# A pairwise scan's key products on another engine, its levels spaced wider, and one weight tile moved by 192 bytes, in a one-core encoder layer

## The chip, the core and the metric

The kernel runs on one core of a Trainium2 chip. The core has five engines that take their instructions in order, each from its own queue, and meet by semaphores: TensorE (PE in the profile; its weight loads are PEld), VectorE (DVE), ScalarE (ACT), GpSimd (POOL) and SyncE (SP), which issues most DMAs here. The metric is the device time of one execution in microseconds, the median of several runs.

## What is computed

One layer of an encoder over 512 tokens of width 1024, in float32. Three branches share one input projection; their results are gated and summed, and a SwiGLU feed-forward part (FFN) of width 2816 follows:

```python
h = rms_norm(x, norm1_g[l])
proj = h @ w_in[l]
u_pool, aq, ak, av, rq, rf, rb, ri, rg, gate_pre = split_cols(proj)
y_pool = pool_mixer(u_pool, pool_w[l], pool_scale[l])
y_attn = diff_attention(aq, ak, av, lam, diff_norm_g[l], lambda_init)
y_rec = hgrn2_mixer(rq, rf, rb, ri, rg, lb_all[0, l], lb_all[1, l], hgrn_norm_g[l])
...
x = x + merged @ w_out[l]
h2 = rms_norm(x, norm2_g[l])
gu = h2 @ w_ffn_in[l]
x = x + (jax.nn.silu(gu[..., :FFN_HIDDEN]) * gu[..., FFN_HIDDEN:]) @ w_ffn_out[l]
```

The branch that matters most here is `hgrn2_mixer`: for 4 heads, in both directions of time, a gated linear recurrence S_t = diag(f_t) S_(t-1) + k_t v_t with key k = 1 - f and output S_t^T q_t. Written without the state, token t weighs the value of token s with the sum over channels of q_t k_s times the product of the gates f between s and t.

## The kernel before, in words

**Precision.** Dense products are made as three passes in the fast format fp32r: activations and weights are each split into a high part and a rest, and high x high, rest x high and high x rest are added up in PSUM. A weight tile comes by DMA as `raw`, ScalarE casts it into `whi` (line 180), and VectorE subtracts to get `wlo` (line 181); `split_w` does this, for 128 x 1024 numbers at a time. Three pairs of such tiles exist at once (pool `wsp`).

**Order.** TensorE's order is fixed by the program, not by a scheduler. `Pipe` keeps a clock of TensorE that `mm` advances by a modelled time for each matmul (about 0.215 us for 512 columns), and switches between several generators. A generator that yields `("w", us)` is resumed no earlier than that many modelled microseconds later, and one that yields `("e", event, us)` that long after an event was marked. Meanwhile the stream of dense jobs (`Jobs.stream`) is served, which yields after every two matmuls. So a number in a `yield` says how many dense matmuls stand between two steps of a scan, and it is not a wait on the chip. The other engines get their instructions in the order in which this program writes them, with some reordering by the scheduler.

**Stages.** The recurrent branch comes first (to about 231 us), then attention (to 366), pooling and the gates and up-projections, the output projection (522 to 568), the FFN's first half in 22 pairs of column tiles (569 to 784) and its second (784 to 905).

**The scan.** `rec_scan(h)` computes one head's 512 x 512 weights by doubling: at level n = 1, 2, 4, ... 128 all pairs of tokens in neighbouring blocks of n get their weights from four matmuls of 128 columns (float32, each shown as two records), "rc<-kq,kc" in the profile, line 90. Their left operand up to n = 64 is `kc`, a copy of the keys with the two directions interleaved (`key_copy`, ScalarE, line 724); the right one is the queries in `kq`. Then the level prepares the next: the queries are multiplied by gate products (two instructions on VectorE, line 755), the keys likewise (one instruction, line 758, on GpSimd for n < 128 and on VectorE for n = 128), the next `key_copy` is made from them, the pyramid of gate products `pyr` grows by a step (VectorE, line 765), and the level's weights are copied under a mask into `pt` (VectorE, line 770). The last pair of blocks, n = 256, needs four matmuls of 256 columns. Every level ends with a yield of 2.0 modelled us, the last with 1.7 (line 774).

**Values jobs.** `values_job` makes the recurrent and the attention branch's values: for each half of 256 columns and each of 4 token blocks, 24 matmuls of 256 columns ("mm<-whi,hT_hi" and the like), whose moving operand is the weight tile and whose stationary one is the transposed input `hT`. `quarter_parts` names their weights.

**Attention.** `att_front_job` evacuates the keys of a head from PSUM, with low halves "l" at line 848, and marks the event `AF`; `att_head` begins its first scores 3.5 modelled us later (line 861).

**FFN pairs.** For each pair j of column tiles `ffn_pair_bodies` runs seven products of 12 matmuls of 256 columns. The activations there stand 192 bytes further on than a tile of a multiple of 256 would, by pads that the program allocates (`h2_a`, `forms_a`). In the first part of pairs 4 and 12 two more matmuls of 512 columns write a PSUM bank that nobody reads ("tp<-whi"; called dummy matmuls below).

Of the kernel before, what the change touches and what calls it, by code (L numbers as in the profile page):

```python
# [11 lines left out]
F32 = mybir.dt.float32  # L12
# [6 lines left out]
P = 128  # L19
# [57 lines left out]
def encoder_kernel(ctx: ExitStack, tc: tile.TileContext, x, norm1_g, w_in, pool_w, pool_scale,  # L77
# [32 lines left out]
    wsp = ctx.enter_context(pool("wsp", 3))  # L110
    small = ctx.enter_context(pool("small", 6))
    psum = ctx.enter_context(pool("psum", 3, space=PSUM))
# [17 lines left out]
    masks = const.tile([P, len(LEVELS), P], U8, name="masks")  # L130
    vecs = const.tile([14, P], F32, name="vecs")
    vcol = const.tile([P, 14], F32, name="vcol")
# [30 lines left out]
    class Part:  # L163


        def __init__(self, chunk, view, a, b, wpool=None):
            self.chunk, self.view, self.a, self.b, self.wpool = chunk, view, a, b, wpool
            chunk.left += 1
# [4 lines left out]
        def split(self):  # L173
            self.hi, self.lo = split_w(self.view(self.chunk.raw), self.a, self.b, self.wpool)
            self.chunk.left -= 1

    def split_w(view, a, b, wpool=None):
        hi = (wpool or wsp).tile([P, a, b], F32R, name="whi")
        lo = (wpool or wsp).tile([P, a, b], F32R, name="wlo")
        nc.scalar.copy(out=hi, in_=view)  # L180
        nc.vector.tensor_tensor(out=lo, in0=view, in1=hi.bitcast(F32), op=ALU.subtract)  # L181
        return hi, lo
# [205 lines left out]

    def quarter_parts(w, c0, n, where=None):

        v = w.rearrange("(kt p) c -> p kt c", p=P)
        for c in range(0, n, 256):
            ch = Chunk(v[:, :, c0 + c:c0 + c + 256], KT, 256, where if c == 0 else None)
            yield slice(c, c + 256), [Part(ch, lambda raw, j=j: raw[:, j:j + 4, :], 4, 256) for j in (0, 4)]

# [71 lines left out]
    xraw = st0.enter_context(pool("xraw", 3))  # L467
    g_b = xg.tile([P, D], F32, name="g1b")
    with tc.issue_after(warmed):
        nc.scalar.dma_start(out=g_b, in_=norm1_g.broadcast_to([P, D]))  # L470
# [238 lines left out]
    def rec_scan(h):  # L709
# [30 lines left out]
        while n < 256:  # L740
            nb2 = S // (2 * n)
            ps = bank("rc", (P, NB, P))
            for b in range(NB):
# [6 lines left out]
                mm(ps[:, b, :], ks, qs, True, True)  # L750

            for off, o in ((0, tstep + 1), (S + n, 0)):
                xv = strided(kq, off, [[2 * n, nb2], [1, n]])
                tv = strided(tot, toff + o, [[2, nb2], [0, n]])
                nc.vector.tensor_tensor(out=xv, in0=xv, in1=tv, op=ALU.mult)  # L755
            xv = strided(kq, 2 * S, [[2 * n, nb2], [S + n, 2], [1, n]])
            tv = strided(tot, toff + 1, [[2, nb2], [tstep - 1, 2], [0, n]])
            (nc.gpsimd if n < 128 else nc.vector).tensor_tensor(out=xv, in0=xv, in1=tv, op=ALU.mult)  # L758
            if n < 64:
                kc = key_copy(2 * n)  # L760
            if n < 128:
# [11 lines left out]
            n *= 2  # L773
            yield ("w", 2.0 if n <= 128 else 1.7)
        for d in range(2):
# [21 lines left out]
    cols["rg"] = col_parts(w_in2, KT, OFF["rg"], 512, P)  # L797
    vparts = list(quarter_parts(w_in2, OFF["ri"], 512))

# [58 lines left out]
    def att_head(h):  # L858
        if h:
            yield ("e", f"T{h - 1}", 0.0)  # L860
        yield ("e", f"AF{h}", 3.5)
        t = att.pop(h)
# [74 lines left out]
    add_att(1)  # L937
    aparts = list(quarter_parts(w_in2, OFF["av"], 512))
    for i, (cs, parts) in enumerate(aparts):
# [174 lines left out]
    def ffn_pair_bodies(j):  # L1114
# [3 lines left out]
        def first(part):  # L1118
# [7 lines left out]

            if j in (4, 12):
                w = part.hi.rearrange("p n k c -> p (n k c)")
                for skip in (0, 16):
                    mm(bank("tp"), w[:, 0:P], w[:, skip:skip + 512], True, True)  # L1130
# [241 lines left out]
```

## Time and profile before

| | us |
|---|---|
| median of 3 runs | 913.66 |
| lowest and highest | 913.07, 913.75 |
| the profiled execution | 913.64 |
| its span, first to last instruction | 911.9 |
| TensorE busy | 889.2 (98%) |
| VectorE busy | 582.0 (64%) |
| ScalarE busy | 420.7 (46%) |
| GpSimd busy | 62.0 (7%) |

The busy times are sums over the span and overlap each other, so they don't add up to it. An engine that is busy nearly all the time sets the time, unless its work can be made shorter or it waits less; of an engine that is seldom busy it matters only whether another one waits for its results. A timeline row gives a start, a duration and, in brackets, how long the engine had been idle before it and what ended that idle time. Since matmuls are pipelined, the duration of a row of matmuls is longer than the distance to the next row's start; times per matmul are best taken from starts.

### The profile page before, as it was taken

What the parts mean: (1) busy time and instruction counts of PE and PEld (TensorE: products, weight loads), DVE (VectorE), ACT (ScalarE), POOL (GpSimd) and SP (SyncE); (2) the same over time, 40 slices, a digit from 0 to 9 for tenths busy, and PEclk for the clock granted to TensorE, in tenths of its full rate; (3) what the DMA queues carried; (4) which work ended last, traced back from release to release, by engine and by line L of the source; (5) the groups of instructions that cost most, each with busy time, mean ns of one, the idle gap of its engine ahead of it and who ended that gap; (6) DMA issues with size and microseconds to landing.
All of it is one profiled execution on the core that took longest, in us unless ns stands there. A gap on an engine that the chain in (4) does not pass through costs nothing. (4 is left out here: it accounts for less than half of the span.)

```text
span 911.9 us, 13179 instructions
## 1 busy us (share of the span) xinstructions
PE 889.2 (98%) x5357; PEld 783.6 (86%) x5357; DVE 582.0 (64%) x876; ACT 420.7 (46%) x652; POOL 62.0 (7%) x62
## 2 busy tenths in 40 slices
PE   6999999999999999999999999999999999999996
PEld 5977987887898888778888898999999999888885
DVE  5696553663867765654325554998887888644544
ACT  5544423433655674332233424755655556533433
POOL 2233311210000000000000000000000000000000
PEclk9999999999999999999999999999999999999999
DMA  8322030314033213523334350153433434323312
GB/s 244 106 69 70 3 91 25 114 47 154 26 112 91 89 52 117 185 79 96 97 122 147 102 153 0 48 139 94 137 95 104 128 94 133 122 70 105 111 39 93
DMA packets 106313, 89.01 MB, mean 98 GB/s; under 512 B 2686, under 2 KB 93324, under 8 KB 106124
## 3 DMA queue, kind: packets, MB, share of 16 engines
q1 hardware_dynamic: 105532, 86.59, 31.0%
q10 hardware_dynamic: 720, 1.57, 0.5%
q8 instruction: 42, 0.69, 0.3%
q14 instruction: 19, 0.16, 0.1%
HBM read 86.06 MB, written 2.10 MB: 97 GB/s over the span
## 5 line engine op out<-in xcount | busy, mean ns | idle before, releaser
L181 DVE TENSOR_TENSOR wlo<-raw,whi 128x1024 fp32r<-128x1024 f32 (+1 forms) x146 | 170.2, 1169 | 165.5 <-PE mm L90 85.0
L180 ACT CAST whi<-raw 128x1024 fp32r<-128x1024 f32 (+1 forms) x146 | 143.7, 990 | 207.5 <-PE mm L90 122.1
L90 PE MATMUL mm<-hT_hi,whi 128*128 128x512 f32 (+1 forms) x440 | 110.7, 389 | 0.0
L90 PE MATMUL mm<-hT_hi,wlo 128*128 128x512 f32 (+1 forms) x440 | 108.3, 383 | 0.0
L90 PE MATMUL mm<-hT_lo,whi 128*128 128x512 f32 (+1 forms) x440 | 107.9, 382 | 0.0
L90 PEld LDWEIGHTS mm<-hT_hi,whi 128*128 128x128 f32 x440 | 79.2, 191 | 16.0 <-issue 1.9
L90 PEld LDWEIGHTS mm<-hT_lo,whi 128*128 128x128 f32 x440 | 79.2, 188 | 15.0
L90 PEld LDWEIGHTS mm<-hT_hi,wlo 128*128 128x128 f32 x440 | 78.9, 188 | 15.4 <-issue 1.0
L299 DVE TENSOR_TENSOR slo<-sums,shi 128x1024 fp32r<-128x1024 f32 x42 | 51.1, 1217 | 0.2 <-ACT shi L297 0.2
L297 ACT CAST shi<-sums 128x1024 fp32r<-128x1024 f32 x42 | 44.2, 1052 | 2.0 <-DVE sums L261 1.5
L758 POOL TENSOR_TENSOR kq<-kq,pyr 128x512 f32<-128x512 f32 x24 | 33.4, 1392 | 46.4 <-ACT kc L724 29.9
L90 PEld LDWEIGHTS rc<-kq,kc 128*128 128x128 f32 x224 | 29.7, 191 | 6.7 <-issue 2.4
L90 PE MATMUL rc<-kq,kc 128*128 128x128 f32 x224 | 32.1, 287 | 2.9 <-DVE kq L755 2.9
L755 DVE TENSOR_TENSOR kq<-kq,pyr 128x256 f32<-128x256 f32 x56 | 26.1, 507 | 13.1 <-PE rc L90 13.0
L724 ACT COPY kc<-kq 128x512 f32<-128x512 f32 x28 | 18.7, 667 | 30.1 <-POOL kq L758 19.0
L882 ACT ACTIVATE s<-s,mx 128x512 f32<-128x512 f32 x32 | 23.0, 720 | 16.2 <-DVE mx L880 16.0
L90 PE MATMUL mm<-fhi,slo 128*128 128x256 f32 x168 | 26.2, 278 | 0.5 <-DVE slo L299 0.5
L90 PE MATMUL mm<-y_hi,whi 128*128 128x512 f32 x96 | 26.4, 393 | 0.0
L90 PE MATMUL mm<-y_lo,whi 128*128 128x512 f32 x96 | 26.2, 392 | 0.0
L90 PE MATMUL mm<-fhi,shi 128*128 128x256 f32 x168 | 26.1, 277 | 0.1
L90 PE MATMUL mm<-flo,shi 128*128 128x256 f32 x168 | 25.9, 276 | 0.0
L90 PE MATMUL mm<-y_hi,wlo 128*128 128x512 f32 x96 | 25.9, 390 | 0.0
(255 smaller groups left out, 1812.0 us busy)
## 6 DMA issues: line engine op xcount, KB each, us to landing
raw<-in_w_ffn_in_dram SPq DMA_DIRECT2D x44, 512.0 KB, 5.2
raw<-in_w_in_dram SPq DMA_DIRECT2D x18, 1024.0 KB, 5.1
raw<-in_w_in_dram SPq DMA_DIRECT2D x24, 512.0 KB, 4.1
raw<-in_w_ffn_out_dram SPq DMA_DIRECT2D x10, 1024.0 KB, 5.1
raw<-in_w_out_dram SPq DMA_DIRECT2D x4, 1024.0 KB, 5.4
xin<-in_x_dram SPq DMA_DIRECT2D x4, 512.0 KB, 9.4
raw<-in_w_up_rec_dram SPq DMA_DIRECT2D x2, 1024.0 KB, 7.9
x<-in_x_dram SPq DMA_DIRECT2D x1, 2048.0 KB
```

Source lines behind the costliest of these rows:

```text
L90: i = nc.tensor.matmul(out_, lhsT=lhsT, rhs=rhs, start=start, stop=stop, skip_group_check=chain)
L180: nc.scalar.copy(out=hi, in_=view)
L181: nc.vector.tensor_tensor(out=lo, in0=view, in1=hi.bitcast(F32), op=ALU.subtract)
L297: nc.scalar.copy(out=hi, in_=view)
L299: on_dve = nc.vector.tensor_tensor(out=lo, in0=view, in1=hi.bitcast(F32), op=ALU.subtract).ins
L724: nc.scalar.copy(out=strided(kc, 0, [[2 * n, S // (2 * n)], [n, 2], [1, n]]), in_=strided(kq, 2 * S, [[2 * n, S // (2 * n)], [S + n, 2], [ ...
L755: nc.vector.tensor_tensor(out=xv, in0=xv, in1=tv, op=ALU.mult)
L758: (nc.gpsimd if n < 128 else nc.vector).tensor_tensor(out=xv, in0=xv, in1=tv, op=ALU.mult)
L882: nc.scalar.activation(out=s, in_=s, func=AF.Exp, scale=-1.0, bias=mx[:, c:c + 1], accum_out=zz[:, i, c:c + 1])
```

## The change

1. In a level of the scan, the key product goes to VectorE for all n. It is written ahead of the two query products, and `key_copy` right behind it.
2. The yields between levels become 2.7 and 2.4 modelled us.
3. The weights of the values jobs (recurrent `ri` and attention `av`) begin 192 bytes into their tile; for that `wsp` tiles hold 1088 numbers instead of 1024.
4. The first scores of an attention head follow the event `AF` by 4.4 instead of 3.5.
5. The dummy matmuls stay at j = 4 only.
6. The pool of small tiles has 5 buffers instead of 6, and `vecs` lives in a pool of the first stage. With this all the tiles allocated behind `wsp` on that side move by a multiple of 256 bytes.

```diff
-    small = ctx.enter_context(pool("small", 6))
+    small = ctx.enter_context(pool("small", 5))
...
-    vecs = const.tile([14, P], F32, name="vecs")
...
-    def split_w(view, a, b, wpool=None):
-        hi = (wpool or wsp).tile([P, a, b], F32R, name="whi")
-        lo = (wpool or wsp).tile([P, a, b], F32R, name="wlo")
+    def split_w(view, a, b, wpool=None, skip=0):
+
+        n, k = a * b, skip // 4
+        hi, lo = ((wpool or wsp).tile([P, n if wpool else 1088], F32R, name=name)[:, k:k + n]
+                  .rearrange("p (a b) -> p a b", a=a) for name in ("whi", "wlo"))
         nc.scalar.copy(out=hi, in_=view)
         nc.vector.tensor_tensor(out=lo, in0=view, in1=hi.bitcast(F32), op=ALU.subtract)
...
+    vecs = xg.tile([14, P], F32, name="vecs")
...
+            xv = strided(kq, 2 * S, [[2 * n, nb2], [S + n, 2], [1, n]])
+            tv = strided(tot, toff + 1, [[2, nb2], [tstep - 1, 2], [0, n]])
+            nc.vector.tensor_tensor(out=xv, in0=xv, in1=tv, op=ALU.mult)
+            if n < 64:
+                kc = key_copy(2 * n)
             for off, o in ((0, tstep + 1), (S + n, 0)):
                 xv = strided(kq, off, [[2 * n, nb2], [1, n]])
                 tv = strided(tot, toff + o, [[2, nb2], [0, n]])
                 nc.vector.tensor_tensor(out=xv, in0=xv, in1=tv, op=ALU.mult)
-            xv = strided(kq, 2 * S, [[2 * n, nb2], [S + n, 2], [1, n]])
-            tv = strided(tot, toff + 1, [[2, nb2], [tstep - 1, 2], [0, n]])
-            (nc.gpsimd if n < 128 else nc.vector).tensor_tensor(out=xv, in0=xv, in1=tv, op=ALU.mult)
-            if n < 64:
-                kc = key_copy(2 * n)
...
-            yield ("w", 2.0 if n <= 128 else 1.7)
+            yield ("w", 2.7 if n <= 128 else 2.4)
...
-    vparts = list(quarter_parts(w_in2, OFF["ri"], 512))
+    vparts = list(quarter_parts(w_in2, OFF["ri"], 512, None, 192))
...
-        yield ("e", f"AF{h}", 3.5)
+        yield ("e", f"AF{h}", 4.4)
...
-    aparts = list(quarter_parts(w_in2, OFF["av"], 512))
+    aparts = list(quarter_parts(w_in2, OFF["av"], 512, None, 192))
...
-            if j in (4, 12):
+            if j == 4:
```

`quarter_parts` and `Part` hand the new argument `skip` on to `split_w`.

The order of the instructions differs from the one before in the stage of the scan, at the first scores of attention and at j = 12. Three places, with the rows of an engine as they stand in its queue. In these rows a name ahead of the arrow is what is written, the names behind it are what is read, and "x4" means four in a row.

TensorE at the end of head 0's scan, before: the three groups "rc<-..." are levels n = 64, n = 128 and the last pair of blocks, with dense matmuls "mm<-..." between them.

```order
L90 MATMUL rc<-kq,kc 128x128 x4
L90 MATMUL mm<-hT_hi,wlo 128x512 x8
L90 MATMUL mm<-hT_hi,whi 128x512 x2
L90 MATMUL rc<-kq 128x128 x4
L90 MATMUL mm<-hT_hi,whi 128x512 x6
L90 MATMUL mm<-hT_lo,whi 128x512 x2
L90 MATMUL rc<-kq 128x256 x4
```

The same place after the change.

```order
L90 MATMUL rc<-kq,kc 128x128 x4
L90 MATMUL mm<-hT_hi,wlo 128x512 x8
L90 MATMUL mm<-hT_hi,whi 128x512 x6
L90 MATMUL rc<-kq 128x128 x4
L90 MATMUL mm<-hT_hi,whi 128x512 x2
L90 MATMUL mm<-hT_lo,whi 128x512 x8
L90 MATMUL mm<-hT_hi,wlo 128x512 x2
L90 MATMUL rc<-kq 128x256 x4
```

Between the levels stand 14 and 12 dense matmuls where 10 and 8 stood.

VectorE at the first levels of head 0, before: "kc<-kq" is the sum of both directions' keys, "wlo" a weight split, "x2" at line 755 the two query products of a level, "pt" the masked copy, "pyr" a step of the gate products.

```order
L717 TENSOR_TENSOR kc<-kq 128x512
L181 TENSOR_TENSOR wlo<-raw,whi 128x1024
L755 TENSOR_TENSOR kq<-kq,f 128x256 x2
L770 COPY_PREDICATED pt<-masks,rc 128x4x128
L765 TENSOR_TENSOR pyr<-pyr 128x2x128
L765 TENSOR_TENSOR pyr<-pyr 128x2x64
L755 TENSOR_TENSOR kq<-kq,pyr 128x128x2 x2
L770 COPY_PREDICATED pt<-masks,rc 128x4x128
```

The same place after the change, where line 757 is the key product and line 763 the query product (768 is the pyramid, 773 the masked copy, 182 the split).

```order
L720 TENSOR_TENSOR kc<-kq 128x512
L757 TENSOR_TENSOR kq<-kq,f 128x256x2
L182 TENSOR_TENSOR wlo<-raw,whi 128x1024
L757 TENSOR_TENSOR kq<-kq,pyr 128x128x2x2
L768 TENSOR_TENSOR pyr<-pyr 128x2x128
L757 TENSOR_TENSOR kq<-kq,pyr 128x64x2x4
L763 TENSOR_TENSOR kq<-kq,f 128x256 x2
L773 COPY_PREDICATED pt<-masks,rc 128x4x128
```

Three levels' key products stand ahead of the first level's query products, since they need no matmul of their level.

TensorE at the first scores of attention, before: the four rows "rc<-k,q" and "rc<-l,q" are the scores (the numbers are those of the tiles), the others a dense job.

```order
L90 MATMUL mm<-hT_lo,whi 128x512 x8
L90 MATMUL mm<-hT_hi,wlo 128x512 x2
L90 MATMUL rc<-k_1865,q_1863 128x512
L90 MATMUL rc<-l_1867,q_1863 128x512
L90 MATMUL rc<-k_1866,q_1864 128x512
L90 MATMUL rc<-l_1868,q_1864 128x512
L90 MATMUL mm<-hT_hi,wlo 128x512 x6
```

The same place after the change.

```order
L90 MATMUL mm<-hT_lo,whi 128x512 x8
L90 MATMUL mm<-hT_hi,wlo 128x512 x6
L90 MATMUL rc<-k_1865,q_1863 128x512
L90 MATMUL rc<-l_1867,q_1863 128x512
L90 MATMUL rc<-k_1866,q_1864 128x512
L90 MATMUL rc<-l_1868,q_1864 128x512
L90 MATMUL mm<-hT_hi,wlo 128x512 x2
```

The scores stand four dense matmuls later.

## Rows read from the trace of the kernel before

**Rows 1.** Page, busy times of the engines and the granted clock in 40 slices.

```profile
PE 889.2 (98%) x5357; PEld 783.6 (86%) x5357; DVE 582.0 (64%) x876; ACT 420.7 (46%) x652; POOL 62.0 (7%) x62
...
PEclk9999999999999999999999999999999999999999
```

**Rows 2.** TensorE's waits: engine, line, waited for; us, times, longest.

```profile
PE rc L90 <- DVE kq L755: 3.5, 5, 1.0
...
PE rc L90 <- DVE kq L758: 1.4, 1, 1.4
PE rc L90 <- DVE l L848: 0.7, 1, 0.7
```

**Rows 3.** Timeline of TensorE, head 0's last levels: start, us, what, idle before.

```profile
64.76 1.13 PE L90 MATMUL rc<-kq 128*128 128x128 f32 x8 [0.52 <-DVE kq L755]
...
67.12 0.61 PE L90 MATMUL mm<-hT_lo,whi 128*128 128x512 f32 x2
69.14 1.97 PE L90 MATMUL rc<-kq 128*128 128x256 f32 x8 [1.41 <-DVE kq L758]
```

**Rows 4.** Timeline of VectorE, same stretch.

```profile
61.99 2.62 DVE L755 TENSOR_TENSOR kq<-kq,pyr 128x256 f32<-128x256 f32 x2
...
65.15 2.57 DVE L181 TENSOR_TENSOR wlo<-raw,whi 128x1024 fp32r<-128x1024 f32 x1
67.65 0.75 DVE L755 TENSOR_TENSOR kq<-kq,pyr 128x256 f32<-128x256 f32 x2
68.32 0.68 DVE L758 TENSOR_TENSOR kq<-kq,pyr 128x512 f32<-128x512 f32 x1
```

**Rows 5.** Groups of VectorE, 380 to 900 us: busy us, mean ns.

```profile
L181 DVE TENSOR_TENSOR wlo<-raw,whi 128x1024 fp32r<-128x1024 f32 x76 | 92.8, 1223 | 120.4 <-PE mm L90 61.1 <-ACT whi L180 59.1
```

**Rows 6.** Timeline of GpSimd, same stretch as rows 4.

```profile
62.22 2.11 POOL L758 TENSOR_TENSOR kq<-kq,f 128x512 f32<-128x512 f32 x1 [6.83 <-ACT whi L180]
65.11 1.52 POOL L758 TENSOR_TENSOR kq<-kq,pyr 128x512 f32<-128x512 f32 x1 [0.79 <-ACT kc L724]
```

**Rows 7.** Busy time in windows of the scan.

```profile
75.00:100.00 25.00, 24.13 (x153) 21.25 (x153) 21.28 (x39) 9.40 (x15) 11.06 (x7) 1.00 0.08 22
```

**Rows 8.** Timeline of TensorE, a values job in the scan.

```profile
95.32 1.12 PE L90 MATMUL mm<-wlo,hT_hi 128*128 128x256 f32 x8
96.28 1.06 PE L90 MATMUL rc<-kq,kc 128*128 128x128 f32 x8
```

**Rows 9.** Timeline of TensorE, FFN, pairs j=4 and j=12.

```profile
614.22 0.63 PE L90 MATMUL rc<-h_hi,wlo 128*128 128x256 f32 x4
614.69 0.64 PE L90 MATMUL tp<-whi 128*128 128x512 f32 x2
615.16 0.63 PE L90 MATMUL mm<-fhi,shi 128*128 128x256 f32 x4
...
691.33 0.63 PE L90 MATMUL tp<-whi 128*128 128x512 f32 x2
691.79 0.63 PE L90 MATMUL mm<-fhi,shi 128*128 128x256 f32 x4
```

**Rows 10.** Groups of GpSimd, whole span, by form.

```profile
L758 POOL TENSOR_TENSOR kq<-kq,pyr 128x512 f32<-128x512 f32 x24 | 33.4, 1392 | 46.4 <-ACT kc L724 29.9 <-DVE pyr L765 14.4 <-DVE kq L755 2.2
L758 POOL TENSOR_TENSOR kq<-kq,f 128x512 f32<-128x512 f32 x4 | 8.7, 2181 | 51.5 <-ACT whi L180 26.5 <-DVE kc L717 18.4 <-DVE sg L704 6.6
```

**Rows 11.** Groups of VectorE, 36 to 206 us, by form.

```profile
L181 DVE TENSOR_TENSOR wlo<-raw,whi 128x1024 fp32r<-128x1024 f32 x19 | 26.5, 1406 | 25.4 <-PE mm L90 14.8 <-ACT pt L735 6.0 <-ACT whi L180 2.8
...
L758 DVE TENSOR_TENSOR kq<-kq,pyr 128x512 f32<-128x512 f32 x4 | 2.7, 682 | 0.0
```

**Rows 12.** Timeline of TensorE, first attention scores.

```profile
231.88 0.39 PE L90 MATMUL rc<-k,q 128*128 128x512 f32 x1
232.92 0.50 PE L90 MATMUL rc<-l,q 128*128 128x512 f32 x1 [0.66 <-DVE l L848]
```

**Rows 13.** Timeline of VectorE, same place.

```profile
231.47 1.40 DVE L848 TENSOR_TENSOR l<-mm,k 64x512 fp32r<-64x512 f32 x2 [1.24 <-ACT k L846]
```

More of the change, by code (lines that the diff above doesn't have):

```diff
@@ L163, in encoder_kernel, with __init__ @@
     class Part:
-        def __init__(self, chunk, view, a, b, wpool=None):
-            self.chunk, self.view, self.a, self.b, self.wpool = chunk, view, a, b, wpool
+        def __init__(self, chunk, view, a, b, wpool=None, skip=0):
+            self.chunk, self.view, self.a, self.b, self.wpool, self.skip = chunk, view, a, b, wpool, skip
             chunk.left += 1
@@ L173, in split @@
         def split(self):
-            self.hi, self.lo = split_w(self.view(self.chunk.raw), self.a, self.b, self.wpool)
+            self.hi, self.lo = split_w(self.view(self.chunk.raw), self.a, self.b, self.wpool, self.skip)
             self.chunk.left -= 1
-    def split_w(view, a, b, wpool=None):
-        hi = (wpool or wsp).tile([P, a, b], F32R, name="whi")
-        lo = (wpool or wsp).tile([P, a, b], F32R, name="wlo")
+    def split_w(view, a, b, wpool=None, skip=0):
+        n, k = a * b, skip // 4
+        hi, lo = ((wpool or wsp).tile([P, n if wpool else 1088], F32R, name=name)[:, k:k + n]
+                  .rearrange("p (a b) -> p a b", a=a) for name in ("whi", "wlo"))
         nc.scalar.copy(out=hi, in_=view)
@@ L387, in row_parts, with quarter_parts @@
                 yield Part(ch, lambda raw, j=j: raw[:, j:j + 2, :], 2, 512, wpool)
-    def quarter_parts(w, c0, n, where=None):
+    def quarter_parts(w, c0, n, where=None, skip=0):
         v = w.rearrange("(kt p) c -> p kt c", p=P)
@@ L393, in quarter_parts @@
             ch = Chunk(v[:, :, c0 + c:c0 + c + 256], KT, 256, where if c == 0 else None)
-            yield slice(c, c + 256), [Part(ch, lambda raw, j=j: raw[:, j:j + 4, :], 4, 256) for j in (0, 4)]
+            yield slice(c, c + 256), [Part(ch, lambda raw, j=j: raw[:, j:j + 4, :], 4, 256, None, skip)
+                                       for j in (0, 4)]
     def cols_mm(ps, part, r, nk, sub=0, lo_col=0, n=512, r_lo_last=False):
```

## The prediction

> **What bounds the kernel now.** I read the page's busy shares first: TensorE works 98% of the span, the other engines at most 64% [rows 1]. So time can leave in two ways only: TensorE waits less, or a matmul takes less. The span is 911.9 us in a profiled execution of 913.64, so about 1.7 lies around it; the median shown is 913.66. All sums below start from 913.64 and need no correction to the median.
>
> The list of TensorE's waits says how much there is to win by waiting less [rows 2]. Apart from the start of the program, the largest entries are two of the scan's own: 3.5 us in five waits for the query products (line 755) and 1.4 us in one wait for a key product (line 758); then 0.7 us once for the attention keys' low halves (line 848). A wait costs a little more than its idle: two matmuls of 512 columns begin at 67.12, and at 0.227 us each the next could begin at 67.57; it begins at 69.14, which is 1.57 later where the profile counts 1.41 idle [rows 3]. So 0.16 more for each of the six: 4.9 + 6 x 0.16 = 5.9 us in the scan.
>
> Why does a query product come late? VectorE's timeline has two of them at 61.99 that took 2.62 us together, and two at 67.65 that took 0.75; a weight split at 65.15 took 2.57 [rows 4], where 76 of the same form later in the kernel averaged 1.223 [rows 5]. GpSimd was running a key product at 62.22 for 2.11 us and another at 65.11 for 1.52 [rows 6]. The long VectorE instructions are those that lie beside a GpSimd one. TensorE's waits at 64.76 and 69.14 [rows 3] follow these two pairs: 61.99 + 2.62 = 64.61, and after 65.15 + 2.57 = 67.72 come the last level's query pair and key product, 67.65 + 0.75 and 68.32 + 0.68, which end at 69.00. VectorE had no long queue of its own: it was busy 21.28 of 25 us in the fullest window that I read, with that stretching in it [rows 7].
>
> For matmul prices I compared start distances at one size, 256 columns. In the values job eight of them go from 95.32 to 96.28, 120 ns each [rows 8]. In the FFN four go from 614.22 to 614.69, 117.5 ns each, and after two dummy matmuls at 614.69 the pitch is shorter: between 615.16 and 691.33 stand 8 pairs of 7 products of 12 matmuls, 672 in 76.17 us, 113.4 ns each [rows 9]. In the values job both operands begin at the same offset modulo 256 bytes (32 and 32); in the FFN the moving operand stands 192 further on (224 and 32), by the pad that the kernel has there. The granted clock is at its upper level, 2.4 GHz, in all these slices [rows 1], so the difference is not the clock's.
>
> **Key products to VectorE.** Leaves GpSimd: 24 instructions of 1.392 us and 4 of 2.181, 42.1 us [rows 10]. Comes to VectorE: 28 at the 0.682 that its four of the same form take now [rows 11], 19.1 us. Leaves VectorE: the stretching. For the 19 splits in this stretch that is 19 x (1.406 - 1.223) = 3.5 us [rows 5, 11], and for a pair of query products like that of 61.99 it is 1.9. So VectorE gets at most 15.6 us more work in 170, on an engine that has 3.7 us of 25 free in a full window [rows 7], some 25 us in 170: no bound by sum. The question is order. At a level, the key product of n up to 64 needs the key copy of its own level (ScalarE) and not TensorE, since the matmuls read the copy; it runs early. Behind it on VectorE wait the query products, the pyramid step, the mask copy and now and then a split, so a key copy that is late behind a weight cast on ScalarE delays all of these.
>
> **Levels further apart.** The modelled gap goes from 2.0 to 2.7 us; between the last levels of head 0 stand 14 and 12 dense matmuls where there were 10 and 8. Four more at 0.227 give VectorE 0.91 us more. A level then has 14 x 0.227 = 3.2 us of cover, or 12 x 0.227 = 2.7; it needs a key product 0.68, two query products 0.75, and a split of 1.22 if one stands ahead: 2.65 if all of it waited for the level's matmuls, and only the queries do. I walked the changed order with these durations. The least room left is about 1.0 us, in head 0's last levels and in head 1 where two splits stand ahead of the queries at n=32, of which the first begins ahead of the level's matmuls. That says all six waits go; I leave 0.4 for what the walk cannot see, and give the residual 0 to 2.5. Term: -5.5 (-5.9 to -3.4). The cover is dense work that has to be done anyway, and the scan doesn't run out of it: a head begins when its front is done, and in the changed order 70 dense matmuls (15.9 us) still stand between the last step of head 3 and the first scores of attention, 72 in the order before. So the spacing costs nothing; if that cover were gone, each level would cost its 0.9 openly.
>
> **Attention's first scores.** The fourth score matmul could begin at 231.88 + 0.227 = 232.11 and begins at 232.92, and the next record is 0.11 longer [rows 12]; it waits for two evacuations at 231.47 that take 1.40 [rows 13]. The delay of 0.9 puts four more dense matmuls ahead, 0.91 us, and the evacuation ends at 232.87, before 233.02. Term: -0.9 (-0.8 to -0.9). Nothing is late next: the later scores run without a stop.
>
> **Value weights 192 bytes on.** 2 sets x 2 halves x 4 blocks x 24 = 384 matmuls go from offsets 32/32 to 224/32. No row shows this pair in this stage, so bounds from the nearest: 113.4 ns as after 615.16, or 117.5 as ahead of 614.69. That is 384 x 6.6 = 2.5 or 384 x 2.5 = 0.9; no row of 256 columns is above 120, so no loss. I take 115 between them: -1.9.
>
> The Trainium skill ("SBUF — State Buffer", section "SBUF: two separate sides") says the opposite: on the engines' side of SBUF only the port pair that VectorE and GpSimd share is contended for, and TensorE waits for nobody. By it an offset would be worth nothing and the term would be 0, which is R2 below. The trace has 120 against 113.4 for one size, so I follow the rows.
>
> **Dummy matmuls at j=12.** Two matmuls, 691.33 to 691.79, 0.46 us on TensorE's path [rows 9]. Term: -0.5 (-0.4 to -0.5). Whether the 113.4 ns hold without them is R3.
>
> **Priced at nothing.** One buffer fewer in the pool of small tiles: each is read within its block, and five are left. The tile of vectors goes to another pool; its four loads keep their place. Other tiles move by 768 bytes, a multiple of 256, so offsets that matter stay. GpSimd's remaining work (the powers in the norms) comes earlier, and nobody waits for it at present.
>
> **Sum.** 913.64 - 5.5 - 0.9 - 1.9 - 0.5 = 904.84, say 904.9.
>
> **Rivals.** *Waits stay by order (R1).* In-order VectorE has key product, splits and evacuations ahead of the queries; where the key copy is behind a cast on ScalarE, the queue stands. If half of the 5.9 stays: 913.64 - 2.95 - 3.3 = 907.4. For it: two levels whose room is only about 1 us. Against it: the waits now all lie beside stretched instructions. Chance 0.15.
> *The offset does nothing (R2)*, as if 120 ns came from the values job itself: 904.9 + 1.9 = 906.8. For it: no row isolates the offset. Chance 0.08.
> *The FFN falls back (R3).* The change does less than it says if the FFN pays for it. The step from 117.5 to 113.4 at 614.69 looks like a state that two dummy matmuls set. If the pair at j=4 no longer sets it and no second pair follows, the stretch from 615 to 784 goes at 0.470 per four instead of 0.4525: 169 x 3.9% = 6.5, so 911.4. Against it: their addresses modulo 256 do not change. Chance 0.04.
> *Slower: VectorE becomes the bound of the scan (R4).* A level with two splits ahead that all wait for its matmuls needs 0.68 + 0.75 + 2 x 1.22 = 3.87 against a cover of 2.7 to 3.2, some 0.9 late. If half of the 28 levels were so, the waits would be 14 x 0.9 = 12.6 in place of 5.9: 913.64 + 6.7 - 3.3 = 917.0. It turns into a loss where waits pass 5.9 + 3.3 = 9.2 us, 0.33 a level. For it: 21.28 busy of 25 in one window. Against it: the stretching that leaves, and that 19 splits stand in this stretch, few of them in pairs. Chance 0.06.
>
> **How the numbers follow.** Forecast 0.67, R1 0.15, R2 0.08, R3 0.04, R4 0.06. The low end: every term at its best is 9.8 us, 903.8, and 0.4 more if the slow state before 614.69 is shorter: 903.4. The high end: 3.4 + 0.8 + 0.9 + 0.4 = 5.5 off, 908.1, which takes in R2 and most of R1; 908.2. About 2 in 10 is left outside. A measurement here can tell some 0.2%, 1.8 us. Faster by more: forecast, R1, R2 and half of R3, 0.92; within: the other half of R3 and the mild part of R4, 0.04; slower: the rest of R4, 0.04.
>
> **What would show it.** Right: no entry above 0.5 us for the query products in TensorE's waits and none for line 848 at the first scores; VectorE's splits in the scan back at 1.22 mean; values matmuls eight in 0.91 to 0.94 us; after the pair at j=4 four in 0.4525. Wrong: query waits of 0.3 us or more at many levels (R4), few long ones behind splits (R1), values still at 0.96 for eight (R2), FFN at 0.47 (R3). What would upset the forecast most is a queue on VectorE that a late key copy holds, since everything of a level is behind it.

## The result, and the profile after

The changed kernel took 904.12 us (median of 13 executions, 903.43 to 911.20), the kernel before beside it 914.07 (13, 912.71 to 922.35): a ratio of 0.9888, 95% interval 0.9853 to 0.9923. The interval is wide because the executions of either kernel fall into two groups some 7 us apart: 903.43 to 904.35 (eight) and 910.79 to 911.20 (five) here, 912.71 to 914.07 (seven) and 920.02 to 922.35 (six) before. Group against group the change is -9.7 us (medians 903.91 against 913.65) and -9.8 (911.07 against 920.90). What the groups are is taken up in the section on them below. The profiled executions, 903.87 and 913.64 us, both belong to the lower group; their spans are 902.0 and 911.9. Forecast were 904.9 us, and 903.4 to 908.2.

Where the time went is read from the starts of TensorE's rows at six places that both kernels have: the scan's first level, attention's first score, the first pooled product, the output projection's first matmul, the FFN's first, and the FFN's second half. This is TensorE's timeline of the kernel before at these places (start, duration, what).

```profile
40.39 0.82 PE L90 MATMUL rc<-kq,kc 128*128 128x128 f32 x4
...
231.42 0.39 PE L90 MATMUL rc<-k,q 128*128 128x512 f32 x1
...
378.00 1.02 PE L90 MATMUL rc<-dpool,pw 128*128 128x512 f32 x2
...
522.33 0.87 PE L90 MATMUL mm<-whi,m_hi 128*128 128x256 f32 x6
...
568.91 0.62 PE L90 MATMUL mm<-h_hi,whi 128*128 128x256 f32 x4
...
784.28 0.39 PE L90 MATMUL rc<-whi,shi 128*128 128x512 f32 x1
```

And of the changed kernel; the row at 605.35 is the pair of dummy matmuls at j = 4, which stands at 614.69 in [rows 9].

```profile
40.29 0.99 PE L90 MATMUL rc<-kq,kc 128*128 128x128 f32 x5
...
224.39 0.39 PE L90 MATMUL rc<-k,q 128*128 128x512 f32 x1
...
368.74 1.02 PE L90 MATMUL rc<-dpool,pw 128*128 128x512 f32 x2
...
513.04 0.87 PE L90 MATMUL mm<-whi,m_hi 128*128 128x256 f32 x6
...
560.18 0.62 PE L90 MATMUL mm<-h_hi,whi 128*128 128x256 f32 x4
...
605.35 0.63 PE L90 MATMUL tp<-whi 128*128 128x512 f32 x2
...
774.46 0.39 PE L90 MATMUL rc<-whi,shi 128*128 128x512 f32 x1
```

| stretch of TensorE | before, us | after, us | difference |
|---|---|---|---|
| scan, to the first score | 191.03 | 184.10 | -6.93 |
| attention, to pooling | 146.58 | 144.35 | -2.23 |
| pooling, gates, up-projections | 144.33 | 144.30 | -0.03 |
| output projection | 46.58 | 47.14 | +0.56 |
| FFN to the dummies at j = 4 | 45.78 | 45.17 | -0.61 |
| from there to the FFN's second half | 169.59 | 169.11 | -0.48 |

The four dense matmuls that now stand ahead of the first scores (0.91 us) moved from the second stretch to the first, so the scan's own gain is 7.84 and attention's 1.32.

The list of TensorE's waits of the changed kernel has none of the three entries of [rows 2]; this is the whole list (engine, line, what for; us, times, longest). The first two belong to the program's start.

```profile
PE tp L98 <- DVE hrow L432: 7.3, 1, 7.3
PE rc L98 <- DVE hrow L432: 1.4, 1, 1.4
PE mm L90 <- DVE slo L300: 0.4, 1, 0.4
```

VectorE's groups in the scan, 36 to 206 us, by form (busy us, mean ns):

```profile
L182 DVE TENSOR_TENSOR wlo<-raw,whi 128x1024 fp32r<-128x1024 f32 x20 | 24.2, 1218 | 16.0 <-ACT whi L181 6.8 <-PE mm L90 4.4 <-ACT pt L784 3.8
...
L757 DVE TENSOR_TENSOR kq<-kq,pyr 128x512 f32<-128x512 f32 x28 | 19.1, 683 | 2.2 <-ACT kc L727 1.8
```

The splits average 1.218 us where they had 1.406 [rows 11], and the 28 key products 0.683. The window that was VectorE's fullest [rows 7] now reads as follows (TensorE busy 25.00 of 25.00, VectorE 17.87, GpSimd 0.00):

```profile
75.00:100.00 25.00, 25.00 (x187) 23.81 (x186) 17.87 (x35) 10.02 (x17) 0.00 (x0) 1.00 0.08 22
```

Of these 28 key products 24 are new on VectorE, and with them come the four of the first levels, which took 1.138 us each: 20.9 us of work more. Yet its busy time over the whole span grew by 4.3 us only (582.0 to 586.3), and in this window, which does not hold quite the same work in both kernels, it is 3.4 us lower: the stretched rows are gone, query products among them (0.507 us before, 0.420 now). The last levels of head 0, which began after 0.52 and 1.41 us of idle [rows 3], begin without any:

```profile
69.37 1.05 PE L90 MATMUL rc<-kq 128*128 128x128 f32 x8
...
72.99 1.67 PE L90 MATMUL rc<-kq 128*128 128x256 f32 x7
```

### The profile page after: what moved, and what is told of

The parts are those of the page before. It is cut to its first block, busy times and chain, and to the rows that moved or that the text cites. A ratio compares the mean times of both kernels' runs of the same rounds, so it can differ in the third digit from the quotient of the medians.

```text
span 902.0 us, 13155 instructions
## 1 busy us (share of the span) xinstructions
PE 885.1 (98%) x5355; PEld 782.7 (87%) x5355; DVE 586.3 (65%) x904; ACT 420.8 (47%) x652; POOL 19.4 (2%) x34
## 3 DMA queue, kind: packets, MB, share of 16 engines
q10 hardware_dynamic: 720, 1.57, 0.5%
## 4 chain that ended last, share of the span: by engine, by line
PE 94%; DVE 3%; DMA 1%; ACT 1%; issue 1%; POOL 0%; POOLq 0%; SPq 0%; ACTq 0%; DVEq 0%
PE mm L90 66%; PE rc L90 23%; PE tp L90 4%; PE tp L98 2%; DMA xin<-in_x_dram 1%; DVE hid L352 1%; DMA raw<-in_w_ffn_in_dram 0%; DVE flo L352 0%; DVE h_lo L451 0%; DVE wlo L182 0%; DVE slo L300 0%; DVE hrow L432 0%; PE rc L98 0%; ACT x L1218 0%; ACT hrow L426 0%
## 5 line engine op out<-in xcount | busy, mean ns | idle before, releaser
L182 DVE TENSOR_TENSOR wlo<-raw,whi 128x1024 fp32r<-128x1024 f32 (+1 forms) x146 | 166.5, 1144 | 154.9 <-PE mm L90 77.7
L763 DVE TENSOR_TENSOR kq<-kq,pyr 128x256 f32<-128x256 f32 x56 | 21.5, 420 | 25.6 <-PE rc L90 25.5
L90 PE MATMUL mm<-whi,hhi 128*128 128x512 f32 x66 | 25.7, 389 | 0.0
```

Source lines behind the costliest of these rows:

```text
L90: i = nc.tensor.matmul(out_, lhsT=lhsT, rhs=rhs, start=start, stop=stop, skip_group_check=chain)
```

## Experiments on the scan

Three kernels undo the two parts of the scan's change, together and singly.

**Both undone.** Key product on GpSimd again (for n < 128, but written ahead of the queries), spacing 2.0 and 1.7:

```diff
-            nc.vector.tensor_tensor(out=xv, in0=xv, in1=tv, op=ALU.mult)
+            (nc.gpsimd if n < 128 else nc.vector).tensor_tensor(out=xv, in0=xv, in1=tv, op=ALU.mult)
...
-            yield ("w", 2.7 if n <= 128 else 2.4)
+            yield ("w", 2.0 if n <= 128 else 1.7)
```

> The changed kernel with its scan as it was in two points: key product for n<128 back on GpSimd (still written ahead of the queries) and spacing 2.0/1.7. Everything else stays changed. Theory (GpSimd's product stretches the VectorE instructions beside it, and the narrow spacing doesn't cover that): TensorE waits of 4 to 6 us for kq are back, 4 to 6 us slower than the changed kernel, that is 908 to 910. Rival (the position ahead of the queries was what helped): no waits above 0.5 us, within 1 us of the changed kernel.

Measured: 912.63 us median (lower group 911.97 to 913.39). Its waits:

```profile
PE rc L90 <- DVE kq L763: 3.8, 5, 1.3
PE mm L90 <- ACT shi L298: 1.5, 1, 1.5
...
PE rc L90 <- DVE kq L757: 1.0, 1, 1.0
```

Six waits of 4.8 us are back, and the stretch from the scan's first level to the first score takes 190.91 us, 6.8 more than in the changed kernel. That is more than the 4 to 6 expected. The position ahead of the queries, which this kernel keeps, helped little: less the four dense matmuls that moved (0.91) and with the value weights' 0.76 put back, the stretch would be 190.76 us against 191.03 before, 0.3 less. The rest of the difference isn't the scan's: 0.8 us fell at the program's start and 1.5 in the FFN, where the cast of the second row stood behind another that waited 2.40 us for its weight load (0.92 in the changed kernel). The third kernel has this wait too (1.0 us), the other ten and the two under study don't. Why the load was later there was not found.

**Only the engine undone.** The first of the two edits alone; TensorE's order is that of the changed kernel.

> The changed kernel with the key product for n<128 back on GpSimd; spacing 2.7/2.4 stays, TensorE's order is unchanged. Theory 1 (both parts are needed, each covers some): VectorE's splits in the scan back at 1.35 to 1.4 us mean, TensorE waits 1 to 3 us in the scan, 905 to 907. Rival A (the spacing alone covers everything): the same stretching on VectorE but no waits, within 0.3 us of the changed kernel. Rival B (the engine is all): the whole 4 to 6 us come back.

Measured: 904.22 us median (four executions, 903.98 to 904.94). In TensorE's waits there is no entry for kq. VectorE's splits, and GpSimd's key products:

```profile
L182 DVE TENSOR_TENSOR wlo<-raw,whi 128x1024 fp32r<-128x1024 f32 x20 | 27.4, 1380 | 18.2 <-ACT whi L181 6.8 <-PE mm L90 4.5 <-ACT pt L784 3.8
```

```profile
L757 POOL TENSOR_TENSOR kq<-kq,pyr 128x512 f32<-128x512 f32 x24 | 29.6, 1234 | 59.4 <-ACT kc L727 45.9 <-DVE pyr L768 10.6 <-DVE kq L763 2.9
```

Rival A holds: GpSimd runs its 38 us of key products (29.6 and 8.4 for the four first levels), VectorE's splits are stretched (1.380 us), and TensorE waits for none of it. From the scan's first level to the first score it took 184.37 us against 184.10. With the wide spacing the move to VectorE is worth 0.3 us, if anything.

**Only the spacing undone.** The second edit alone; key products on VectorE.

> The changed kernel with spacing 2.0/1.7; key products stay on VectorE. Theory 1 (both parts are needed): VectorE's splits at 1.22 mean, but 10 dense matmuls are 2.27 us against 0.75 of queries and 1.22 of a split: TensorE waits 0.5 to 2.5 us in the scan, 0.5 to 3 us slower than the changed kernel. Rival B (the engine is all): no waits, within 0.3 us. Rival A (the spacing is all): 4 to 6 us come back.

Measured: 906.59 us median (lower group 905.19 to 906.92). Its waits:

```profile
PE mm L90 <- ACT shi L298: 1.0, 1, 1.0
PE rc L90 <- DVE kq L763: 0.6, 1, 0.6
```

VectorE's splits average 1.222 us, unstretched, and yet one wait of 0.6 us stays (the starts of TensorE's rows show a second of 0.26); the stretch to the first score is 185.33 us, 1.2 more than in the changed kernel, and 1.0 of the rest is the load in the FFN. So either edit alone takes most of the waits: the engine 5.6 of the 6.8 us that both undone cost, the spacing 6.5. They are two ways to the same gain, not two gains.

## Experiments on the other three terms

**Attention's first scores.**

```diff
-        yield ("e", f"AF{h}", 4.4)
+        yield ("e", f"AF{h}", 3.5)
```

> The changed kernel with attention's first scores 3.5 modelled us behind the event as before. Forecast's term: a wait of 0.65 to 0.7 us for line 851 (the low halves of the keys) at the first scores is back, 0.9 us slower: 904.8. Rival (with the scan's waits gone VectorE is earlier there, so that the wait doesn't come back): no difference.

Measured: 904.42 us median (904.19 to 904.59). TensorE's timeline at the first scores:

```profile
224.27 0.39 PE L90 MATMUL rc<-k,q 128*128 128x512 f32 x1
225.31 0.50 PE L90 MATMUL rc<-l,q 128*128 128x512 f32 x1 [0.66 <-DVE l L851]
```

The wait is back to the hundredth [rows 12]: 225.31 - 224.27 - 0.227 = 0.81. The median is 0.5 us above the changed kernel's lower group; in the trace scan and attention together take 0.8 us more (329.22 against 328.45). The rival falls.

**The offset of the value weights.** First at the tile's start, then 64 bytes on; the second has the instructions in the same order as the changed kernel.

```diff
-    vparts = list(quarter_parts(w_in2, OFF["ri"], 512, None, 192))
+    vparts = list(quarter_parts(w_in2, OFF["ri"], 512, None, 0))
...
-    aparts = list(quarter_parts(w_in2, OFF["av"], 512, None, 192))
+    aparts = list(quarter_parts(w_in2, OFF["av"], 512, None, 0))
```

> The changed kernel with the value weights at the start of their tile again (offsets 32/32 modulo 256). Theory: the 384 values matmuls go back from 117 ns to 120 ns, 1.2 us slower (the term of the forecast was 0.9 to 2.5), and nothing else moves. Rival (the offset does nothing, the 117 ns come from other tiles' places): values stay at 117 ns, no difference. Second rival: later stages change too, since the out projection has 118 ns in the changed kernel where it had 113 to 114 before, and the FFN ahead of pair 4 has 113 where it had 117; if the values jobs hand on what sets these, out goes back to 113 to 114 (-0.9 us) and the FFN ahead of pair 4 to 117 (+0.6 us).

> The changed kernel with the value weights 64 bytes into their tile (offsets 96/32 modulo 256) instead of 192 (224/32); the order of the instructions is the same. Theory 1 (what counts is only that the two offsets differ): the values matmuls stay at 117 ns or go to 113, as with 192, time as the changed kernel within 0.5 us. Theory 2 (the distance counts): a third pitch, or 120 ns as with offset 0 and 0.7 to 1.2 us slower.

Measured: 904.86 us median at offset 0 (lower group 904.60 to 905.09), 903.87 at 64 (903.58 to 903.87). TensorE's timeline in a values job at offset 0, then at 64:

```profile
93.30 1.12 PE L90 MATMUL mm<-whi,hT_lo 128*128 128x256 f32 x8
...
95.22 0.40 PE L90 MATMUL mm<-whi,hT_hi 128*128 128x256 f32 x2
```

```profile
93.41 1.10 PE L90 MATMUL mm<-whi,hT_lo 128*128 128x256 f32 x8
...
95.29 0.40 PE L90 MATMUL mm<-whi,hT_hi 128*128 128x256 f32 x2
```

And in the changed kernel, at 192, in the same job, on either side of a scan level:

```profile
93.04 1.07 PE L90 MATMUL mm<-whi,hT_lo 128*128 128x256 f32 x8
...
94.85 0.39 PE L90 MATMUL mm<-whi,hT_hi 128*128 128x256 f32 x2
...
96.68 1.10 PE L90 MATMUL mm<-whi,hT_lo 128*128 128x256 f32 x8
...
98.56 0.64 PE L90 MATMUL mm<-whi,hT_hi 128*128 128x256 f32 x4
```

Between the two rows of a pair stand 16 matmuls: 1.92 us at offset 0, 120 ns each; 1.88 at 64, 118 ns each; at 192 it is 1.81 ahead of the level, 113 ns each, and 1.88 behind it. By the starts of the single matmuls the recurrent values at 192 go on like this, 113.5 and 117.8 ns in turn in all their eight stretches between scan levels (115.6 on average), while at 64 all eight have 117.7 to 118.0. Attention's values have mostly the slower pitch at both (117.0 and 116.7 on average). Over the scan and attention the kernel at offset 0 took 0.76 and 0.40 us more than the changed one, 1.16 in all; the kernel at 64 bytes took 0.40 more and 0.10 less. So it counts that the offsets differ, which is worth 0.9 us at 64 bytes and 1.2 at 192, and in the scan the distance counts as well, by the one profile at 64. That the kernel at 64 bytes has the changed one's time all the same comes from its output projection (46.6 us against 47.1), which is taken up below. The output projection and the FFN ahead of j = 4 at offset 0 are as in the changed kernel (47.13 and 45.19 us), so the second rival falls.

**The second pair of dummies.**

```diff
-            if j == 4:
+            if j in (4, 12):
```

> The changed kernel with the second dummy pair at j = 12 back. Forecast's term: 0.46 us slower in the lower group, nothing else. Rival (the second pair is a second chance to leave 117.5 ns): the upper group lies only some 2.5 to 3.5 us above the lower one, since the pairs behind j = 12 run at 113 ns. Second rival (each pair flips the pitch): fast executions become slow behind j = 12.

Measured: 904.23 us median (903.91 to 904.48). From the dummies at j = 4 to the FFN's second half TensorE took 169.59 us, to the hundredth what it took before, and 0.48 more than without the pair. So the second pair did not flip the pitch, and the second rival falls. No execution of four lay in the upper group, so the first rival is not decided.

## Experiments on the two groups of executions

**No dummies at all** (`if j == 4` made never true).

> The changed kernel without any dummy matmuls (the pair at j = 4 is gone too). Executions of the changed kernel fall into two groups, 903.4 to 904.4 us and 910.8 to 911.2 us. Theory (the 7 us are the FFN's 256-column matmuls at 117.5 instead of 113.4 ns, and the dummy pair switches between the two): without the pair the FFN keeps the pitch with which it starts, so that the shares of the two groups change; in a profile with 113 ns ahead of pair 4, the rest of the FFN stays at 113 and the time is 0.5 us below the changed kernel's lower group; with 117.5 ahead, it stays at 117.5 and the time is 6.5 us above. Rival (the groups have another cause, another stage): the shares stay about 8 to 5, and the time falls by the pair's 0.46 us in both.

Measured: 902.83, 903.21, 903.97 and 910.62 us, and the profiled execution is the last of these. It is the only profile of an upper group other than those of the kernels with single dummies below:

```profile
605.04 0.63 PE L90 MATMUL rc<-h_lo,whi 128*128 128x256 f32 x4
605.52 0.63 PE L90 MATMUL rc<-h_hi,wlo 128*128 128x256 f32 x4
...
700.21 0.63 PE L90 MATMUL rc<-h_hi,slo 128*128 128x256 f32 x4
700.68 0.52 PE L90 MATMUL mm<-fhi,whi 128*128 128x256 f32 x3
```

And the changed kernel, in the lower group, in the same part of the FFN:

```profile
700.12 0.62 PE L90 MATMUL rc<-h_lo,whi 128*128 128x256 f32 x4
700.57 0.62 PE L90 MATMUL rc<-h_hi,wlo 128*128 128x256 f32 x4
```

Four matmuls take 0.47 us throughout in the one and 0.45 in the other. From the first FFN matmul on transformed inputs to the FFN's second half it is 206.24 us against 199.49, 6.75 more although the pair is left out; with the pair's 0.46 that is the distance of the groups, 7.2. So in this kernel the upper group is the FFN's pitch, 117.7 instead of 113.4 ns for 256 columns, at one clock level (mean granted clock 0.998 in both); that it is so in the two kernels under study is likely, since their groups lie as far apart (7.2 us), but not shown: none of their upper executions was profiled. In this execution the slower pitch stood from 591 us, behind the last wait, to the FFN's end. Both groups exist without dummies, so that the dummies alone don't make them.

**One dummy in each of nine pairs, two in each of nine pairs.**

```diff
-            if j == 4:
+            if 4 <= j <= 12:
...
-                for skip in (0, 16):
+                for skip in (0,):
```

> The changed kernel with one dummy matmul of 512 columns in the first part of each pair j = 4 to 12, nine in all, in place of two at j = 4. It is to show what a dummy does to the pitch of the FFN's 256-column matmuls (113.4 or 117.7 ns, which hold for a whole stage until something disturbs them: without dummies the 117.7 held from 591 us to the FFN's end). Cost of the dummies 9 x 0.23 - 0.46 = 1.6 us: lower group 905.5. Theory 1 (a dummy leads from 117.7 to 113.4 and never back): no pitch of 117.7 behind a dummy, no upper group. Theory 2 (a dummy draws the pitch anew or flips it): stretches of both behind j = 4, all executions between 905 and 912, no two groups. Theory 3 (a dummy does nothing): two groups 6.7 us apart as before.

> The same with the pair of dummies (the second reads 64 bytes further on) in each of the pairs j = 4 to 12. Cost 8 x 0.46 = 3.7 us: lower group 907.6. Theory 1 (a pair leads to 113.4 and never back): no upper group, all executions within 1 us. Theory 2 (drawn anew or flipped): stretches of both pitches behind j = 4, executions spread between 907 and 913. Theory 3 (nothing): two groups 6.7 us apart.

Measured: 912.45 us median with one (eleven executions, 911.46 to 913.30), 907.50 with two (five, 907.10 to 907.60). Timeline of the first at its first dummy:

```profile
604.85 0.62 PE L90 MATMUL rc<-h_hi,wlo 128*128 128x256 f32 x4
605.30 0.39 PE L90 MATMUL tp<-whi 128*128 128x512 f32 x1
605.53 0.63 PE L90 MATMUL mm<-fhi,shi 128*128 128x256 f32 x4
606.00 0.40 PE L90 MATMUL mm<-flo,shi 128*128 128x256 f32 x2
```

A group of four takes 0.45 us ahead of the dummy and 0.47 behind it: a single dummy at the tile's start switches the FFN to the slow pitch, and it stays there behind all nine. All eleven executions are in an upper group by that. With pairs the pitch stays at 113.4 behind all nine, and all five executions are in a lower one (907.50 is 903.9 plus 3.6 for eight more pairs). None of the three theories of a single dummy had it: it leads from the fast pitch to the slow one.

**A single dummy at the other offset, and the two in turn.**

```diff
-                for skip in (0, 16):
+                for skip in (16,):
```

```diff
-            if j == 4:
+            if j in (4, 6, 8, 10):
...
-                for skip in (0, 16):
+                for skip in (0 if j in (4, 8) else 16,):
```

> The changed kernel with a single dummy matmul at j = 4, the one whose moving operand begins 64 bytes into the tile (the first one, which begins at its start, is left out). Single dummies at the tile's start led to 117.7 ns behind each of nine and pairs to 113.4. Theory 1 (the last matmul's moving offset decides the pitch that follows): 113.4 ns behind it, all executions in one group at 903.7, 0.23 below the changed kernel's lower group. Theory 2 (a single one disturbs, whatever its offset): 117.7 ns behind it, 910.3 to 911. Theory 3 (chance): both groups.

> The changed kernel with single dummies at j = 4, 6, 8 and 10, in turn at the tile's start (j = 4 and 8) and 64 bytes into it (j = 6 and 10). Theory 1 (the offset decides): the pitch goes to 117.7 ns at j = 4, to 113.4 at j = 6, to 117.7 at j = 8 and to 113.4 at j = 10; two stretches of two column pairs at 0.8 us a pair more, 907.6 with the dummies' 0.46. Theory 2 (a single one disturbs, whatever its offset): 117.7 ns from j = 4 to the end, 910.5 to 911.5. Theory 3 (the pitch is kept by the first): no change behind j = 4.

Measured: the first of the two took 910.66 us median (twelve executions, 909.83 to 910.99, all in the upper group), the second 905.69 (four, 905.41 to 906.50). Timeline of the first at its dummy, then of the second at its dummies at j = 4 and 6:

```profile
605.40 0.63 PE L90 MATMUL rc<-h_hi,wlo 128*128 128x256 f32 x4
605.87 0.40 PE L90 MATMUL tp<-whi 128*128 128x512 f32 x1
606.11 0.63 PE L90 MATMUL mm<-fhi,shi 128*128 128x256 f32 x4
606.58 0.52 PE L90 MATMUL mm<-flo,shi 128*128 128x256 f32 x3
```

```profile
605.05 0.62 PE L90 MATMUL rc<-h_hi,wlo 128*128 128x256 f32 x4
605.50 0.39 PE L90 MATMUL tp<-whi 128*128 128x512 f32 x1
605.74 0.63 PE L90 MATMUL mm<-fhi,shi 128*128 128x256 f32 x4
606.21 0.52 PE L90 MATMUL mm<-flo,shi 128*128 128x256 f32 x3
...
625.05 0.63 PE L90 MATMUL rc<-h_hi,wlo 128*128 128x256 f32 x4
625.52 0.40 PE L90 MATMUL tp<-whi 128*128 128x512 f32 x1
625.75 0.62 PE L90 MATMUL mm<-fhi,shi 128*128 128x256 f32 x4
626.21 0.62 PE L90 MATMUL mm<-flo,shi 128*128 128x256 f32 x4
```

In the second the offset seems to decide: four take 0.45 us ahead of the first dummy and 0.47 behind it (605.74 to 606.21), 0.47 ahead of the one at 64 bytes and 0.46 behind it (625.75 to 626.21), 0.47 again at 645.03, and 113.3 ns each on average behind j = 10. (The 0.8 us a pair of columns in the expectation was an error: 84 x 4.3 ns are 0.36, so that four slow pairs and the dummies give some 905.8, as measured.) But the first kernel contradicts it: the slow pitch stood already ahead of j = 4 (605.40 to 605.87), and the dummy at 64 bytes alone left it as it was (606.11 to 606.58). So it took the slow pitch that a dummy at the start had set back to the fast one, and did not do so for the slow pitch that stood there otherwise. Two kinds of slow would explain that; no run separates them, and it stays open. It also stays open why a kernel with the pair at j = 4 has an upper group at all, when in the kernel before the pair led from 117.8 ns to 113.4.

None of these kernels is faster than the changed one by more than its executions scatter: the one without dummies has 902.83 to 903.97 in its lower group, and an upper group as well.

## Why the prediction was right, point by point

The time and the sign were right (904.9 against 904.12), and the measured 904.12 lies inside the range. Two things in this are luck. The median stands for the lower group, which is the one that the prediction started from, because eight of 13 executions fell there; with two more in the upper one it would have been some 910.8, outside the range. And the sum, -8.8 against -9.8, has a term that was too small by 1.6, beyond its own bounds, and one that was too large by 0.7:

| term | forecast | measured | by |
|---|---|---|---|
| scan waits | -5.5 | -7.1 | 7.84 less the first set's values 0.76 |
| first scores | -0.9 | -0.9 (-0.8) | attention 1.32 less the second set's values 0.40 (the kernel that undoes it) |
| value weights | -1.9 | -1.2 | kernel with offset 0 |
| dummies at j = 12 | -0.5 | -0.5 | last stretch |
| output projection | 0 | +0.6 | stage table |
| FFN ahead of j = 4 | 0 | -0.6 | stage table |

**Scan waits.** All went, as the walk through the changed order said; the residual of 0.4 was not there. The term was mis-sized at its price: 4.9 us of idle plus 0.16 for each of six waits, with bounds of -5.9 to -3.4. The starts of the single matmuls in the kernel before show what it left out. The six waits themselves cost 5.8 us, as priced (0.63, 0.68, 1.57, 1.03, 1.16 and 0.75 beyond a step without a wait). Behind each, the next matmul's start comes 0.076 us late, 0.46 in all; the 0.11 of this kind behind the wait at 232.92 [rows 12] was priced at the first scores and left out in the scan. And four steps into a level have a stop of 0.04 to 0.12 us that the list of waits does not carry, each with the same 0.076 behind it, 0.70 in all. Together that is 7.0 of the 7.1 us.

**The reason given for the waits** was half of it. VectorE's stretched rows beside GpSimd were there and are gone, but they are not what has to go: with 14 and 12 matmuls of cover the stretched VectorE is early enough (second kernel), and with the unstretched one 10 and 8 nearly are (third kernel). The prediction took both edits together and so did not see that one covers the other. What it said of the price of spacing, nothing, holds: attention and pooling take 144.30 and 144.33 us with the narrow spacing and 144.35 and 144.30 with the wide one. Its 19.1 us of new work on VectorE were 20.9, since the first levels' key products took 1.138 and not 0.682 us; no wait of TensorE came of it.

**First scores and the dummies** came out as the rows said, each shown singly: 0.8 us by the kernel with the old distance, 0.48 by the one with the second pair.

**Value weights.** The range was 0.9 to 2.5 and the truth 1.2, near the bound from the FFN ahead of j = 4, not between the two. The pitch of 256 columns with different offsets is not one number: it is 113.4 or 117.7 ns, in the recurrent values each half of the time (115.6 on average, near the 115 that was taken) and in attention's mostly the latter (117.0).

**Not forecast:** the output projection at 118 where the kernel before had mostly 113 to 114, and the opposite in the FFN ahead of j = 4. Nothing shows that the change did this: of the twelve kernels above seven have 47.1 to 47.2 us in the output projection and five 46.6 to 46.8, and among the six that differ from the changed one in the FFN's dummies alone four have 47.13 and two 46.70 and 46.77. In all fourteen profiles this stage begins at 117.8 ns. In the eight with 47.1 us and more it stays there; in the other six it falls to 113 to 114 some 7 us in, in five of them right behind a stop of 0.05 to 0.12 us (one of the eight has such a stop too and keeps its pitch). In the FFN ahead of j = 4 the kernel without dummies and the one with a single dummy 64 bytes on have the slow pitch where the changed kernel, the same up to there, has the fast one. The two differences cancel here by luck. Both come from the step of the prediction that took the pitch of a stage as given by the offsets and the dummies.

**The rivals.** R1 (waits stay by VectorE's order) and R4 (VectorE becomes the bound) have no entry in the waits to stand on. R2 falls with the kernel at offset 0: 1.2 us. The Trainium skill ("SBUF — State Buffer", section "SBUF: two separate sides") says that on the engines' side of SBUF TensorE waits for no other engine. That an offset would be worth nothing was the prediction's reading of this. 1.92 against 1.88 us for 16 matmuls that differ in nothing but 64 bytes speaks against that reading; that a matmul waited for another engine it does not show. R3 was right as a mechanism and wrong in its place: the FFN at the slow pitch costs 6.75 us (6.5 were worked out), but it is no price of the change. An upper group occurs in both kernels, in five and six of 13 executions here and in nine of 57 later ones of the kernel before, where R3 had a chance of 0.04.

## What to carry to other kernels

Where an in-order engine is late by some tenths, look first for work of the bounding engine that can be put in between: here four matmuls that had to be done anyway, put between two levels, were worth as much as taking 42 us of key products off GpSimd (6.5 and 5.6 us). Two edits that each cure the same wait must not be priced as a sum, and running each alone tells it. Before a change of some tenths of a per cent is judged, look at whether single executions fall into groups and compare group with group.

## What the runs showed of the hardware

The pitch of 256-column matmuls has three values at one clock level: 120 ns with the weights at the start of their tile, which the prediction gives as 32 modulo 256 bytes for both operands, and 113.4 or 117.7 with the weights 192 or 64 bytes further on. That 256 bytes are the period was not tested. Of the last two a stage can keep one for long, for 170 us of the FFN in the changed kernel (the fast one) and for 190 in the execution without dummies (the slow one). What changes it is shown in part: a level of the scan did so each time in the changed kernel, at 192 bytes (with the narrow spacing not each time), and never in the one profile at 64; a short stop did so in five output projections of six; a single matmul of 512 columns at the tile's start brought the slow one in each case seen (a switch from the fast one at 605.30 and 605.50, and by 645.03), and pairs of them, the second 64 bytes on, left nine times the fast one. That such a state exists, and that it moves a whole execution by 7 us (shown in the kernel without dummies), was not expected; what it is inside TensorE no run shows.
